# Seven-product up-projection of a transformer trunk: the first pair's products in another order, its first weight splits ahead of the activation sums, and the modulation's transposes one step later

## Chip, cores and metric

The kernel runs on one core of a Trainium2 chip. Times are device microseconds (us) of one execution. The core's engines are TensorE (PE, with its weight loads as PEld), VectorE (DVE), ScalarE (ACT), GpSimd (POOL) and SyncE (SP), which issues the DMA transfers. Each engine takes its instructions in order.

## What is computed

One inference step of a two-layer streaming encoder over 1024 prompt positions and 8 x 16 sample positions, model width 1024. Each layer has attention (of two kinds), then a GEGLU channel mixer with a causal convolution of width 3 between its projections. A modulation by `c` (shift, scale and gate, from a linear layer) goes around both. The part that matters here is the channel mixer:

```python
def conv_ffn(h, prev, w_up, conv_w, conv_b, w_down):
    u = h @ w_up
    B, T, C = u.shape
    if prev is None:
        prev = jnp.zeros((B, CONV_W - 1, C), u.dtype)
    ue = jnp.concatenate([prev.astype(u.dtype), u], axis=1)
    y = conv_b
    for tap in range(CONV_W):
        y = y + conv_w[tap] * ue[:, tap:tap + T]
    a, g = jnp.split(y, 2, axis=-1)
    out = (jax.nn.gelu(g) * a) @ w_down
    return out, ue[:, T:]
```

`h` has 1152 rows in all, `w_up` is 1024 x 5632 (22 column blocks of 128 for `a`, 22 for `g`), `w_down` 2816 x 1024. All is float32; a float32 product is made of three matmuls, with each operand split in a high and a low part (`hi`: a cast on ACT, L183; `lo`: a subtraction, mostly on DVE, L194): low times high, high times low, high times high.

## The kernel before

**Pairs.** In each layer, blocks j = 0 and 1 of the up-projection are plain matmuls (`plain`, L312). Blocks 2 to 21 are pairs (`spair`): the `a` and the `g` block of one j are seen as a 2x2 block matrix against a 2x2 split of the activations, and the eight products of such a multiplication are replaced by seven, on sums of blocks (`products`, L1229). A product is 24 matmuls, 12 for each of two column parts (320 and 256 columns), with weights of 128x512 split into `wh` and `wl`. Products 11, 21 and 22 of the first pair take activations as they are (in H); products 2, 3, 4 and 1 need sums of activations. Each product accumulates in one of three pairs of PSUM banks: 11 and 21 share one (21 adds on top of 11), 2, 3 and 4 share the second, 1 and 22 the third. `evict` reads them: product 11 is copied by ACT to `p1` (L1197), 21 by ACT (L1188, in `read`), the others are added by DVE (L1190). As product 21 adds to the bank of product 11, its matmuls wait for the copies of L1197.

**Sums.** `tsums` makes the sums of activations for nine tiles of 128 positions: SP loads the tile (`F<-hD`, L1131), POOL makes two subtractions (L1135, L1136), DVE two (L1137, L1138), and each of three results is split by a cast on ACT (into `xa` or `x2r`) and a subtraction on DVE. A fourth sum, T1S, is gathered over all tiles, and at the end of `tsums` split at once, into a part of H that products 11, 21 and 22 do not read, for product 1 (ACT 128x2304, then DVE). The weights of a pair (L1394, L1395, 512 KB each) are summed by POOL (L1177 to L1180) at the head of `products`, and the split of a product's weights is written ahead of its matmuls. Each of the wide casts and copies on ACT is thus in one queue: the sums' casts, the T1S cast, the weight casts, the convolution's L1299, the copies of L1197.

**Order.** The program is written as Python loops; a scheduling layer then sets each engine's order from the written order, data dependences and priorities (`issue_after`, `high_priority`), and inserts the waits. So a line that moves can shift the order elsewhere.

**Modulation.** `ada` is a generator that is advanced a step at a time (`self.step(1)`, at products 0, 2, 4 and 6 of a pair): sixteen weight loads with small matmuls (L240), two for each of eight steps, then a bias added by DVE (L259) and four transposes on PE (L267), in one step. Four of them run in layer 0's pairs and two in layer 0's attention.

**Tables.** After the first pair of layer 0, `tables_b` (L1789 to L1796) loads a table for the second layer's attention, works on it, writes it out (`eb`) and spreads it by sixteen transfers `skb<-eb` of 393 KB each. They go through SP's queue.

**After the pairs** of layer 1 follows the down-projection `down2` (L1604), whose weights (`in_wdn_dram`) and activations (`actD`) come by DMA. The convolution's ACT part of the last pair (L1340) reads and writes a PSUM bank.

Of the kernel before, what the change touches and what calls it, by code (L numbers as in the profile page):

```python
# [35 lines left out]
NPL = 2  # L36
# [69 lines left out]
class Trunk:  # L106
# [116 lines left out]
    def ada(self, gi, bank, ring=None):  # L223

        nc = self.nc
        ring = ring or self.ws
        ps = self.bank(bank)
        lead = [None] * 4
        for k in range(8):
            for hf in range(2):  # L230
                w = ring.next()
# [29 lines left out]
        if gate is not None:  # L261
            g, hf = gate
            nc.gpsimd.tensor_scalar_add(row[:, 512:768], row[:, hf * 256 : hf * 256 + 256], 1.0)
            for j in range(4):
                nc.sync.dma_start(self.gd[g, :, j * 256 : j * 256 + 256], row[32 * j : 32 * j + 9, 512:768])
        for i in range(4):
            nc.tensor.transpose(ps[:, i * 128 : i * 128 + 128], row[:, i * 128 : i * 128 + 128], self.ident)  # L267
        dst = self.adaT[:, gi * 144 : gi * 144 + 144].rearrange("p (h j i r) -> p h i j r", h=2, j=4, i=2)
# [857 lines left out]
    def tsums(self, ring, order, T1S, TT):  # L1126
        nc = self.nc
        E = nc.vector if len(TT) == 4 else nc.gpsimd
        for t in order:
            s = ring.next()  # L1130
            nc.sync.dma_start(s, self.hD[t])  # L1131
# [3 lines left out]
            E.tensor_sub(x1, b12, b11)  # L1135
            E.tensor_sub(b12, b22, b12)  # L1136
            nc.vector.tensor_sub(b22, b22, x1)  # L1137
            nc.vector.tensor_sub(b21, b21, b22)  # L1138
# [12 lines left out]

    def tviews(self):
# [1 line left out]
        TT = [(X1[:, 0:2304], X1[:, 2304:4608]), (X1[:, 4608:6912], X1[:, 6912:9216]), (X2[:, 0:2304], X2[:, 2304:4608])]  # L1154
        return [[x.rearrange("p (k n) -> p k n", k=4) for x in t] for t in TT]

    def products(self, sa, sg, ua, ug, S, p1s, sub, TT, after, when=None):
        nc = self.nc
        H5 = self.H.rearrange("p a c (t h i) -> p a c t h i", h=2, i=64)

# [13 lines left out]
        S1, S2, S3 = S  # L1174
        a11, a12, a21, a22 = sa[:, 0:512], sa[:, 512:1024], sg[:, 0:512], sg[:, 512:1024]
        E = nc.gpsimd
        E.tensor_add(S1, a21, a22)  # L1177
        E.tensor_sub(S2, S1, a11)
        E.tensor_sub(S3, a11, a21)
        E.tensor_sub(a21, a12, S2)  # L1180

        def read(d, a, ps, n):
            def v(x):
                x = x[:, 0 : NB[n][3] - NB[n][2]]
                return x.rearrange("p (t i) -> p t i", i=64)

            if a is None:
                nc.scalar.copy(d, v(ps))  # L1188
            else:
                nc.vector.tensor_add(d, v(ps), a if len(a.shape) == 3 else v(a))  # L1190

# [20 lines left out]
                if early:  # L1212
                    read(a1, a1, ps, n)

        src = {11: a11, 2: S2, 21: a12, 3: S3, 1: S1, 4: a22, 22: a21}
# [28 lines left out]
    def ffn(self, l, xsrc, xdst, affs):  # L1244
# [142 lines left out]
                    conv_block(ps, j, gg, bi, y[gg][:, bi * 384 : bi * 384 + 384])  # L1387
            gated(j, *y)

        sub = self.subslots(self.wslots[1:4] if l else self.wslots)  # L1390

        def spair(j):
            sa, sg = self.ws.next(), self.ws.next()
            nc.sync.dma_start(sa, I["wup"][l, j])  # L1394
            pairdma = nc.sync.dma_start(sg, I["wup"][l, j + 22]).ins  # L1395
# [16 lines left out]
            self.products(sa, sg, ua, ug, (S1, S2, S3), p1s, sub, TT, after, "first" if j == NPL else None)  # L1412
            ya = yact if l else ys.next()
            row(ua, j, 0, ya)
            gated(j, ya, y[0])
# [7 lines left out]
        self.ws = wide  # L1423
        if l == 0:
            self.bg = [self.ada(g, 7, wide) for g in (3, 4, 5, 6)]
        self.tsums(Ring([F[:, 1536:2560], F[:, 8700:9724], F[:, 11644:12668]]), (0, 1, 2, 3, 4, 8, 5, 6, 7), T1S, TT)
        for u in us.items:
            nc.gpsimd.memset(u[:, 0:2], 0.0)
        for j in range(NPL, NFF):
            spair(j)  # L1430
# [628 lines left out]
```

## Time and profile before

| | |
|---|---|
| median of three runs | 2764.85 us (2760.22 to 2769.29) |
| profiled execution | 2755.46 us, span 2753.7 us |
| mean granted TensorE clock | 0.988 |
| layer 0: plain blocks to pairs | about 524 us |
| layer 1: plain blocks to pairs | about 2026 us |
| layer 1: pairs to down-projection | about 2480 us |

A row of a timeline has start, duration, engine, line, operation, tiles (out <- in), shapes and count, and in brackets the idle time of the engine ahead of it with what ended it. A group's row has busy time and mean duration in ns behind the bar, then idle time ahead of its instructions. A row of waits has the total, the count and the longest. A row of stretches has the window, its length, the busy time of PE, PEld, DVE, ACT and POOL, the granted TensorE clock, the mean share of busy DMA engines and GB/s.

### The profile page before, as it was taken

The numbers are of one execution on the slowest core, as the hardware profiler recorded it, in microseconds if no ns is written. First come the engines' busy times: TensorE is split into PE (matmuls) and PEld (weight loads), VectorE is DVE, ScalarE is ACT, GpSimd is POOL, SyncE is SP. The second block draws the span as 40 slices with busy tenths as digits, with TensorE's granted clock in tenths as the row PEclk, the third lists the DMA queues.
The fourth block names the chain that finished last, engine by engine and source line by source line (L and its number), as shares of the span: only waits on it lengthen the run. The fifth ranks groups of instructions, "written<-read, shape, count | busy, mean of one in ns | idle before, by whom it ended". The sixth has DMA issues, their size and how long they took to land.

```text
span 2753.7 us, 47055 instructions
## 1 busy us (share of the span) xinstructions
PE 2642.9 (96%) x17266; PEld 2342.1 (85%) x17266; DVE 1924.2 (70%) x3836; ACT 1346.8 (49%) x2777; POOL 1066.5 (39%) x775
## 2 busy tenths in 40 slices
PE   7999889999999999999999999989999999998997
PEld 5997768989999998788898888867899999996886
DVE  4376768777666784867754677776787777777568
ACT  3476734433333453543536666662455444455553
POOL 3132623444443467764220121242467656542101
PEclk9999999999999999999999999999999999999999
DMA  8756444564444446765757457773544433348573
GB/s 293 237 159 200 146 132 157 163 233 150 145 149 156 137 141 226 246 212 184 274 200 265 113 158 193 215 216 115 176 147 167 150 135 132 134 152 277 192 240 122
DMA packets 229527, 498.27 MB, mean 181 GB/s; under 512 B 37456, under 2 KB 99232, under 8 KB 229296
## 3 DMA queue, kind: packets, MB, share of 16 engines
q1 hardware_dynamic: 229296, 495.27, 54.7%
q8 instruction: 136, 2.23, 0.3%
q14 instruction: 95, 0.78, 0.1%
HBM read 378.15 MB, written 126.47 MB: 183 GB/s over the span
## 4 chain that ended last, share of the span: by engine, by line
PE 36%; DVE 7%; DMA 3%; issue 2%; ACT 2%; POOL 1%; SPq 0%; DVEq 0%; ACTq 0%; POOLq 0%
PE PS L1229 14%; PE PS L1604 7%; PE PS L325 5%; PE PS L312 4%; PE PS L608 2%; PE PS L586 1%; PE PS L557 1%; DVE wl L194 1%; DVE F L524 1%; DMA w0f<-in_wdn_dram 1%; PE PS L560 1%; DVE xa L194 1%; PE PS L735 1%; DMA H<-actD 0%; DVE x2r L593 0%
## 5 line engine op out<-in xcount | busy, mean ns | idle before, releaser
L1229 PE MATMUL PS<-H,wh 128*128 128x256 f32 (+1 forms) x2288 | 352.8, 295 | 0.0
L1229 PEld LDWEIGHTS PS<-H,wh 128*128 128x128 f32 x2288 | 319.7, 189 | 0.4 <-issue 0.4
L1190 DVE TENSOR_TENSOR F<-PS,F 128x256 f32<-128x256 f32 (+1 forms) x446 | 197.7, 452 | 170.2 <-PE PS L1229 163.2
L183 ACT CAST wh<-F 128x512 fp32r<-128x512 f32 (+3 forms) x224 | 137.8, 625 | 209.7 <-PE PS L1229 94.1
L194 DVE TENSOR_TENSOR wl<-F,wh 128x512 fp32r<-128x512 f32 (+2 forms) x208 | 199.3, 968 | 42.3 <-ACT wh L183 41.7
L1229 PE MATMUL PS<-H,wl 128*128 128x256 f32 (+1 forms) x1144 | 201.8, 297 | 13.0 <-ACT F L1197 6.3
L1229 PEld LDWEIGHTS PS<-H,wl 128*128 128x128 f32 x1144 | 168.9, 190 | 19.0 <-ACT F L1197 6.5
L1229 PE MATMUL PS<-xa,wh 128*128 128x320 f32 (+1 forms) x1152 | 176.2, 294 | 0.0
L1229 PEld LDWEIGHTS PS<-xa,wh 128*128 128x128 f32 x1152 | 159.7, 188 | 0.4 <-issue 0.4
L1472 DVE TENSOR_TENSOR xa<-xa 128x384 fp32r<-128x384 f32 x66 | 97.5, 1489 | 78.2 <-ACT xa L183 74.8
L646 POOL TENSOR_TENSOR F<-F,x2r 64x512 f32<-64x512 f32 x62 | 79.3, 1279 | 163.3 <-DVE F L622 149.4
L1349 POOL TENSOR_TENSOR F<-F 128x1152 f32<-128x1152 f32 x44 | 124.2, 2822 | 47.1 <-DVE F L1342 27.6
L312 PE MATMUL PS<-H,w0r 128*128 128x384 f32 (+1 forms) x720 | 137.2, 341 | 0.0
L325 PE MATMUL PS<-xa,H 128*128 128x512 f32 x504 | 131.1, 402 | 6.2 <-ACT xa L183 3.3
L183 ACT CAST wh<-ws 128x512 fp32r<-128x512 f32 (+1 forms) x120 | 88.9, 747 | 96.0 <-PE PS L1229 39.9
L1278 DVE SCALAR_TENSOR_TENSOR F<-F 128x1024 f32<-128x1024 f32 (+2 forms) x160 | 130.1, 863 | 4.4 <-ACT F L1317 3.1
L312 PE MATMUL PS<-H,wh 128*128 128x384 f32 (+1 forms) x672 | 131.3, 339 | 0.0
L312 PEld LDWEIGHTS PS<-H,w0r 128*128 128x128 f32 x720 | 124.1, 188 | 2.8 <-issue 1.5
L586 PE MATMUL PS<-C,F 128*128 128x128 f32 x720 | 111.6, 279 | 14.6 <-DVE wh L593 5.8
L194 POOL TENSOR_TENSOR wl<-ws,wh 128x1024 fp32r<-128x1024 f32 x28 | 73.1, 2610 | 134.1 <-ACT wh L183 104.0
L325 PEld LDWEIGHTS PS<-xa,H 128*128 128x128 f32 x504 | 95.2, 192 | 28.6 <-ACT xa L183 3.8
L524 DVE CUSTOM_DVE_ANT_0 F<-PS,F,C 128x256 f32<-128x256 f32 (+3 forms) x208 | 97.4, 479 | 30.5 <-PE PS L560 15.0
(360 smaller groups left out, 6988.4 us busy)
## 6 DMA issues: line engine op xcount, KB each, us to landing
ws<-in_adaw_dram SPq DMA_DIRECT2D x64, 512.0 KB
ws<-in_wup_dram SPq DMA_DIRECT2D x49, 512.0 KB
F<-in_adaw_dram SPq DMA_DIRECT2D x48, 512.0 KB
F<-in_wup_dram SPq DMA_DIRECT2D x39, 512.0 KB
actD<-F SPq DMA_DIRECT2D x33, 576.0 KB
ws<-in_wdn_dram SPq DMA_DIRECT2D x33, 512.0 KB
F<-in_wdn_dram SPq DMA_DIRECT2D x33, 512.0 KB
xa<-kH SPq DMA_DIRECT2D x60, 256.0 KB
```

The source lines that it names most:

```text
L183: nc.scalar.copy(out, in_)
L194: self.eng(el).tensor_sub(lo, src, hi.bitcast(F32))
L312: mm = self.nc.tensor.matmul(out[:, 0:n], w[a][:, k * 128 : k * 128 + 128], H[:, p, k, s0 : s0 + n], start=i == 0, stop=i == 23)
L325: self.nc.tensor.matmul(out[:, 0:n], H[:, p, j * kn + k, t0 : t0 + 128], w[a][:, k * n : k * n + n], start=i == 0, stop=i == 23,)
L524: nc.vector.tensor_tensor_reduce(out=p[:, c0 : c0 + w], in0=ps, in1=b, scale=1.0, scalar=init, op0=ALU.add, op1=ALU.min, accum_out=nm)
L586: nc.tensor.transpose(t[:, n * 128 : n * 128 + 128], p[:, (kt - k0) * 128 : (kt - k0) * 128 + 128], self.ident)
L1190: nc.vector.tensor_add(d, v(ps), a if len(a.shape) == 3 else v(a))
L1229: self.pairmm = nc.tensor.matmul(ps[:, 0:m], w[a][:, k * 128 : k * 128 + 128], x(p, k, n), start=start and c == 0, stop=c == 11, skip_grou ...
L1278: nc.vector.scalar_tensor_tensor(o, u, cw[:, cc, i : i + 1], o, op0=ALU.mult, op1=ALU.add)
L1349: nc.gpsimd.tensor_mul(yg, yg, ya)
L1472: nc.vector.tensor_sub(lo, raw, hi.bitcast(F32))
L1604: self.downmm = nc.tensor.matmul(ps, a[p][:, i * 128 : i * 128 + 128], w[q], start=first and c == 0, stop=last and c == 2, skip_group_chec ...
```

## The change

The loads, sums and splits of the first pair's weights (products 11, 22, 21) are written ahead of `tsums`, the raw products run in the order 11, 22, 21, and the split of T1S is written behind product 21's matmuls, to be issued after its evacuation (`tplace`). Two memsets go from POOL to DVE, the first pair skips the modulation steps at its products 0 and 2, and `ada` gives way once more ahead of its transposes. The ring of weight slots starts with another slot. Lines from L267 on have other numbers: L1229 is now L1237, L1197 is L1204, L1188 is L1195, L1131 is L1132, L1299 is L1307, L1340 is L1348, L1604 is L1627, L1796 is L1819.

```diff
@@ ada
+        yield
         for i in range(4):
             nc.tensor.transpose(ps[:, i * 128 : i * 128 + 128], row[:, i * 128 : i * 128 + 128], self.ident)
@@ tsums
-        if len(TT) == 3:
-            H5 = self.H.rearrange("p a c (t h i) -> p a c t h i", h=2, i=64)
+
+    def tplace(self, T1S):
+        H5 = self.H.rearrange("p a c (t h i) -> p a c t h i", h=2, i=64)
+        with self.tc.issue_after(self.evac):
             self.split(T1S, H5[:, 0, 0:4, :, 1, :], H5[:, 1, 0:4, :, 1, :], "a", "v")
@@ products
+    def presum(self, sa, sg, S):
+        E = self.nc.gpsimd
+        S1, S2, S3 = S
+        a11, a12, a21, a22 = sa[:, 0:512], sa[:, 512:1024], sg[:, 0:512], sg[:, 512:1024]
+        E.tensor_add(S1, a21, a22)
+        E.tensor_sub(S2, S1, a11)
+        E.tensor_sub(S3, a11, a21)
+        E.tensor_sub(a21, a12, S2)
+        return {11: a11, 2: S2, 21: a12, 3: S3, 1: S1, 4: a22, 22: a21}
+
-    def products(self, sa, sg, ua, ug, S, p1s, sub, TT, after, when=None):
+    def products(self, sa, sg, ua, ug, S, p1s, sub, TT, after, when=None, src=None, ready={}):
...
+        src = src or self.presum(sa, sg, S)
...
             if a is None:
-                nc.scalar.copy(d, v(ps))
+                self.evac = nc.scalar.copy(d, v(ps)).ins
...
-        order = {None: (11, 2, 21, 3, 1, 4, 22), "first": (11, 21, 22, 2, 3, 1, 4), "last": (11, 2, 3, 1, 4, 21, 22)}[when]
+        order = {None: (11, 2, 21, 3, 1, 4, 22), "first": (11, 22, 21, 2, 3, 1, 4), "last": (11, 2, 3, 1, 4, 21, 22)}[when]
         for i, q in enumerate(order):
-            w = sub.next()
-            self.split(src[q], *w, "a", "v")
+            w = ready.get(q)
+            if w is None:
+                w = sub.next()
+                self.split(src[q], *w, "a", "v")
@@ ffn
-        sub = self.subslots(self.wslots[1:4] if l else self.wslots)
+        sub = self.subslots(self.wslots[3:4] + self.wslots[l:3])
...
-        def spair(j):
+        def spair(j, loaded=None, src=None, ready={}):
...
             def after(i, q):
-                if i % 2 == 0:
+                if j == NPL and i == 2:
+                    self.tplace(T1S)
+                    for u in us.items[1:3]:
+                        nc.vector.memset(u[:, 0:2], 0.0)
+                if i % 2 == 0 and (j > NPL or i > 2):
                     self.step(1)
...
+        first = pairload(NPL)
+        src = self.presum(first[0], first[1], (S1, S2, S3))
+        ready = {}
+        for q in (11, 22, 21):
+            ready[q] = sub.next()
+            self.split(src[q], *ready[q], "a", "v")
         self.tsums(Ring([F[:, 1536:2560], F[:, 8700:9724], F[:, 11644:12668]]), (0, 1, 2, 3, 4, 8, 5, 6, 7), T1S, TT)
-        for u in us.items:
-            nc.gpsimd.memset(u[:, 0:2], 0.0)
+        nc.gpsimd.memset(us.items[0][:, 0:2], 0.0)
```

The engines' orders at the three places that the prediction speaks of. First ACT in layer 1, where the sums end and the first pair begins; `x2r<-F` are casts of the sums, `H<-F 128x36x64` is the T1S cast, `wh<-` are weight casts. Before:

```order
L1299 ACTIVATE F<-PS,F 128x384
L183 CAST x2r<-F 128x4x64
L1291 COPY F<-PS 128x18
L183 CAST x2r<-F 128x4x64
L183 CAST H<-F 128x36x64
L183 CAST wh<-ws 128x512
L1299 ACTIVATE F<-PS,F 128x384
L183 CAST wh<-F 128x512
L1197 COPY F<-PS 128x320
L1197 COPY F<-PS 128x256
```

And with the change, the same place:

```order
L183 CAST x2r<-F 128x4x64
L183 CAST wh<-F 128x512
L1307 ACTIVATE F<-PS,F 128x384
L183 CAST wh<-F 128x512
L1204 COPY F<-PS 128x320
L1204 COPY F<-PS 128x256
L183 CAST wh<-ws 128x512
L1299 COPY F<-PS 128x18
L1356 ACTIVATE F<-F 128x1152
L183 CAST wh<-F 128x512
L1195 COPY F<-PS 128x5x64
L1195 COPY F<-PS 128x4x64
```

The T1S cast has left the rows ahead of the copies of product 11 (L1197, now L1204); it stands directly behind the last row shown, the evacuation of product 21 (L1195). In layer 0 the two copies stand directly behind the last cast of the sums.

Second, SP's queue in layer 0, from the last loads of the sums (`F<-hD`) to the weights of the second pair (`in_wup_dram`). Before:

```order
L1131 DMA F<-hD 128x1024 x2
L232 DMA ws<-in_adaw_dram 128x1024
L1131 DMA F<-hD 128x1024
L1351 DMA actD<-F 128x1152
L232 DMA F<-in_adaw_dram 128x1024 x2
L1789 DMA F<-in_relf_dram 16x257
L1394 DMA F<-in_wup_dram 128x1024
L1351 DMA actD<-F 128x1152
L1792 DMA eb<-F 16x768
L1395 DMA ws<-in_wup_dram 128x1024
L232 DMA F<-in_adaw_dram 128x1024
L1796 DMA skb<-eb 128x1x768 x10
```

With the change:

```order
L1812 DMA ws<-in_relf_dram 16x257
L1132 DMA F<-hD 128x1024
L1815 DMA eb<-ws 16x768
L1132 DMA F<-hD 128x1024
L232 DMA ws<-in_adaw_dram 128x1024
L1819 DMA skb<-eb 128x1x768 x3
L1132 DMA F<-hD 128x1024
L1359 DMA actD<-F 128x1152
L1819 DMA skb<-eb 128x1x768 x3
L232 DMA F<-in_adaw_dram 128x1024
L1819 DMA skb<-eb 128x1x768 x4
L232 DMA F<-in_adaw_dram 128x1024
```

The table's load and the `skb` transfers, which stood behind the second pair's weights, now stand between the last loads of the sums and ahead of those weights (fourteen of the sixteen are ahead of the first one).

Third, PE in layer 1 where the last pair ends and `down2` begins. Before (the last two rows are the last product of the pair, its second column part):

```order
L1229 MATMUL PS<-x2r,wh 128x256 x8
L1229 MATMUL PS<-H,wl 128x320 x4
L1229 MATMUL PS<-H,wh 128x320 x8
L1604 MATMUL PS<-wh,xa 128x512 x3
L1604 MATMUL PS<-wl,xa 128x512
L1604 MATMUL PS<-wh,xa 128x512
...
L1604 MATMUL PS<-wh,xa 128x512
L1229 MATMUL PS<-H,wl 128x256 x4
L1229 MATMUL PS<-H,wh 128x256 x8
```

With the change:

```order
L1237 MATMUL PS<-x2r,wh 128x320 x8
L1627 MATMUL PS<-wh,xa 128x512
L1627 MATMUL PS<-wl,xa 128x512
L1237 MATMUL PS<-x2r,wl 128x256 x4
L1237 MATMUL PS<-x2r,wh 128x256 x8
L1237 MATMUL PS<-H,wl 128x320 x4
L1237 MATMUL PS<-H,wh 128x320 x8
L1627 MATMUL PS<-wh,xa 128x512 x2
...
L1627 MATMUL PS<-wh,xa 128x512
L1237 MATMUL PS<-H,wl 128x256 x4
L1237 MATMUL PS<-H,wh 128x256 x8
```

Two of `down2`'s matmuls now stand ahead of the last two groups of the pair, and 58 more (12 before) ahead of its last twelve matmuls.

More of the change, by code (lines that the diff above doesn't have):

```diff
@@ L1172, in halves @@
             return v.rearrange("p (t h i) -> p t h i", h=2, i=64)[:, :, h, :]
[L1174 to L1180, printed above, removed]
+        src = src or self.presum(sa, sg, S)
         def read(d, a, ps, n):
@@ L1213, in evict @@
                     read(a1, a1, ps, n)
-        src = {11: a11, 2: S2, 21: a12, 3: S3, 1: S1, 4: a22, 22: a21}
         group = {11: 0, 21: 0, 2: 1, 3: 1, 4: 1, 1: 2, 22: 2}
-        order = {None: (11, 2, 21, 3, 1, 4, 22), "first": (11, 21, 22, 2, 3, 1, 4), "last": (11, 2, 3, 1, 4, 21, 22)}[when]
+        order = {None: (11, 2, 21, 3, 1, 4, 22), "first": (11, 22, 21, 2, 3, 1, 4), "last": (11, 2, 3, 1, 4, 21, 22)}[when]
         for i, q in enumerate(order):
-            w = sub.next()
-            self.split(src[q], *w, "a", "v")
+            w = ready.get(q)
+            if w is None:
+                w = sub.next()
+                self.split(src[q], *w, "a", "v")
             x = operand(q)
@@ L1388, in plain, with pairload @@
             gated(j, *y)
-        sub = self.subslots(self.wslots[1:4] if l else self.wslots)
-        def spair(j):
+        sub = self.subslots(self.wslots[3:4] + self.wslots[l:3])
+        def pairload(j):
             sa, sg = self.ws.next(), self.ws.next()
             nc.sync.dma_start(sa, I["wup"][l, j])
-            pairdma = nc.sync.dma_start(sg, I["wup"][l, j + 22]).ins
+            return sa, sg, nc.sync.dma_start(sg, I["wup"][l, j + 22]).ins
+        def spair(j, loaded=None, src=None, ready={}):
+            sa, sg, pairdma = loaded or pairload(j)
             ua, ug = us.next(), us.next()
@@ L1410, in after @@
                     row(ug, j, 1, y[0])
-            self.products(sa, sg, ua, ug, (S1, S2, S3), p1s, sub, TT, after, "first" if j == NPL else None)
+            self.products(sa, sg, ua, ug, (S1, S2, S3), p1s, sub, TT, after, "first" if j == NPL else None, src, ready)
             ya = yact if l else ys.next()
@@ L1425, in ffn @@
             self.bg = [self.ada(g, 7, wide) for g in (3, 4, 5, 6)]
+        first = pairload(NPL)
[4 more added lines that the diff above has]
+            self.split(src[q], *ready[q], "a", "v")
         self.tsums(Ring([F[:, 1536:2560], F[:, 8700:9724], F[:, 11644:12668]]), (0, 1, 2, 3, 4, 8, 5, 6, 7), T1S, TT)
-        for u in us.items:
-            nc.gpsimd.memset(u[:, 0:2], 0.0)
+        nc.gpsimd.memset(us.items[0][:, 0:2], 0.0)
         for j in range(NPL, NFF):
-            spair(j)
+            if j == NPL:
+                spair(j, first, src, ready)
+            else:
+                spair(j)
             if l == 0 and j == 2:
```

## Prediction

> **What bounds the kernel now.** I start on the profile's page, with the busy shares.
>
> ```profile
> span 2753.7 us, 47055 instructions
> PE 2642.9 (96%) x17266; PEld 2342.1 (85%) x17266; DVE 1924.2 (70%) x3836; ACT 1346.8 (49%) x2777; POOL 1066.5 (39%) x775
> L1229 PE MATMUL PS<-H,wl 128*128 128x256 f32 (+1 forms) x1144 | 201.8, 297 | 13.0 <-ACT F L1197 6.3
> ```
>
> TensorE (PE) works 96% of the span, so only its 111 us of idle time (2753.7 - 2642.9), and time at a reduced clock, can be won; the other engines count where PE waits for them. The second row is a group of the seven-product matmuls: the last column says that it lost 13.0 us to idle time, 6.3 of it to the copy on ACT at L1197. The waits grouped by what PE waited for (total, times, longest) show where this comes from.
>
> ```profile
> PE PS L1229 <- ACT F L1197: 8.5, 2, 6.3
> PE PS L1229 <- ACT PS L1340: 5.2, 1, 5.2
> ```
>
> So the copies at L1197 (product 11's evacuation, on whose bank product 21 accumulates) cost two waits, one in each layer's first pair. Next the timeline of PE and ACT (start, duration) at the first, in layer 0.
>
> ```profile
> 523.80 3.04 PE L1229 MATMUL PS<-H,w0r 128*128 128x320 f32 x22
> 526.68 0.75 PE L1229 MATMUL PS<-H,wl 128*128 128x320 f32 x4
> 532.06 4.98 PE L1229 MATMUL PS<-H,w0r 128*128 128x320 f32 x24 [2.20 <-ACT F L1197]
> 536.88 0.28 PE L1229 MATMUL PS<-H,wh 128*128 128x256 f32 x1
> 527.67 0.41 ACT L183 CAST x2r<-F 128x256 fp32r<-128x256 f32 x1
> 527.98 2.12 ACT L183 CAST H<-F 128x2304 fp32r<-128x2304 f32 x1
> 531.59 0.69 ACT L1197 COPY F<-PS 128x320 f32<-128x320 f32 x2
> ```
>
> The copies stand in ACT's queue behind the last cast of the activation sums (527.67) and the 2.12 us cast that splits T1S (527.98). PE has products 11 and 22 and then stands 2.20 us. The 24 matmuls behind the wait take 532.06 to 536.88, 4.82 us; ahead of it 22 of the same took 2.88 (523.80 to the next group's start at 526.68), so 24 would take 3.14. The other 1.68 us are a slower clock: the table of stretches gives it (the number behind POOL's), here and in layer 1.
>
> ```profile
> 532.00:536.00 4.00, 3.94 (x17) 3.94 (x18) 3.66 (x8) 0.55 (x4) 0.36 (x3) 0.58 0.00 0
> 2036.00:2042.00 6.00, 6.00 (x27) 6.00 (x28) 5.54 (x8) 1.27 (x4) 5.38 (x7) 0.55 0.10 21
> ```
>
> Granted clock 0.58 and 0.55, after 2.20 and 6.29 us of idle time. The Trainium skill, "TensorE: Matmul & The Clock Gate", section "What's actually happening", puts the fall to half clock behind an idle window of about 3.4 us; by that, the 2.20 us wait would cost no clock and the sum below would be 1.7 us smaller. The row of 0.58 differs, and I go by it.
>
> Layer 1 is the same place with a dearer wait:
>
> ```profile
> 2026.33 0.74 PE L1229 MATMUL PS<-H,wl 128*128 128x320 f32 x4
> 2028.56 1.10 PE L1229 MATMUL PS<-H,wh 128*128 128x256 f32 x8
> 2035.96 1.44 PE L1229 MATMUL PS<-H,wl 128*128 128x320 f32 x4 [6.29 <-ACT F L1197]
> 2041.65 0.75 PE L1229 MATMUL PS<-H,wl 128*128 128x320 f32 x4
> 2031.57 0.41 ACT L183 CAST x2r<-F 128x256 fp32r<-128x256 f32 x1 [0.16 <-DVE F L1138]
> 2031.88 2.11 ACT L183 CAST H<-F 128x2304 fp32r<-128x2304 f32 x1
> 2033.89 0.61 ACT L183 CAST wh<-ws 128x512 fp32r<-128x512 f32 x1
> 2034.41 0.67 ACT L1299 ACTIVATE F<-PS,F 128x384 f32<-128x384 f32 x1
> 2034.98 0.61 ACT L183 CAST wh<-F 128x512 fp32r<-128x512 f32 x1
> 2035.49 0.69 ACT L1197 COPY F<-PS 128x320 f32<-128x320 f32 x2
> ```
>
> Here only product 11 (24 matmuls, 2026.33 to 2029.66) is there to run; then 6.29 us of nothing, then 24 matmuls in 5.69 us (2035.96 to 2041.65) where 3.33 is normal: 2.36 of clock.
>
> **The change, part by part.** All sums are made against the profiled execution, 2755.46 us; it lies 9.4 under the median of the runs, 2764.85, to which the differences are then applied.
>
> *Layer 1, -7.4.* The T1S cast goes behind product 21's evacuation and product 22 ahead of 21. On ACT there remain, behind the cast of 2031.57, one weight cast, one L1299 and one more weight cast, then the copies. From row to row those three take 1.60 us (2033.89 to 2035.49); so the copies start at 1.6 behind 2031.95 or so, 2033.6, and PE, which started 0.47 after the copies' start (2035.49 to 2035.96), at 2034.0. Its two products now reach from 2026.33 to 2033.0 (twice 3.33). A wait of 1.0 to 1.1 stays, half of what first brought a slow clock above. Saved: 6.29 - 1.1 + 2.36 = 7.55. The T1S split, 2.11 on ACT and as much again on DVE, now stands between the evictions of products 21 and 2, where PE has two products (6.7 us) before it needs what is behind; I take 0.15 of new waiting, bounds 0 and 1.5.
>
> *Layer 0, -3.2.* Products 11 and 22 already ran ahead of 21, so PE needs the copies at 523.80 + 2 x 3.14 = 530.1. The last cast of the sums ended at 528.08, and the copies now follow it directly: with 0.47 to PE that is 528.6, 1.5 us early, if the last tile comes as before. It may not, for the next reason, so 0.7 of wait is taken: -(2.20 - 0.7 + 1.68) = -3.2, bounds -3.9 and 0.
>
> *The skew loads, -3.0.* A side effect: the tables of the second attention now use a weight slot, and their sixteen `skb<-eb` loads stand in SP's queue among the last loads of the sums. Before:
>
> ```profile
> 510.54 3.29 SPq L1131 DMA_DIRECT2D F<-hD  x2
> 518.94 0.32 SPq L1131 DMA_DIRECT2D F<-hD  x1
> 524.77 0.75 POOL L1135 TENSOR_TENSOR F<-F 128x256 f32<-128x256 f32 x1 [3.00 <-DMA F<-hD]
> 538.80 0.33 SPq L1789 DMA_DIRECT2D F<-in_relf_dram  x1
> 539.27 0.33 SPq L1394 DMA_DIRECT2D F<-in_wup_dram  x1
> 545.86 7.75 SPq L1796 DMA_DIRECT2D skb<-eb  x10
> 545.00:573.00 28.00, 26.39 (x216) 24.46 (x215) 17.60 (x29) 8.34 (x15) 10.90 (x7) 1.00 0.97 323
> 578.04 1.47 POOL L1177 TENSOR_TENSOR F<-F 128x512 f32<-128x512 f32 x1 [13.09 <-DMA F<-in_wup_dram]
> 567.27 0.64 PE L240 MATMUL PS<-ws,C 128*32 128x256 f32 x8 [1.61 <-DMA ws<-in_adaw_dram]
> 579.29 0.64 PE L240 MATMUL PS<-F,C 128*32 128x256 f32 x8 [0.68 <-DMA F<-in_adaw_dram]
> 581.38 0.85 PE L1229 MATMUL PS<-H,wl 128*128 128x320 f32 x4 [1.46 <-DVE wl L194]
> ```
>
> They held the DMA engines at 0.97 and 323 GB/s for 28 us, and behind them POOL waited 13.09 us for the third pair's weights and PE 1.61 + 0.68 + 1.46 = 3.75. Started some 25 us earlier, they fall where DMA had gaps: in 532 to 536 the row above has 0.00. I take 3.0 of the 3.75, bounds 0 and -3.75. The price is on the other side: three of the skb loads (393 KB each, 3.65 us at 323 GB/s) now stand ahead of the last load of the sums, which so far took 5.8 us from issue to use (518.94 to 524.77); that is the 0.7 above. Pair 2's weights stand behind fourteen of them, but at that rate these take 17 us from about 520, which ends before the 539.27 at which the first of them was issued so far.
>
> *Layer 1's last pair and the down-projection, -4.5.* The instruction order moves here too, though the diff touches nothing near. Before, the last pair's last twelve matmuls stood 12 matmuls into the down-projection and waited 5.2 us (L1340, quoted).
>
> ```profile
> 2481.10 0.96 PE L1604 MATMUL PS<-wh,xa 128*128 128x512 f32 x3 [1.59 <-ACT wh L183]
> 2490.69 1.19 PE L1229 MATMUL PS<-H,wl 128*128 128x256 f32 x4 [5.23 <-ACT PS L1340]
> 2490.00:2500.00 10.00, 8.60 (x28) 7.17 (x29) 7.40 (x14) 6.03 (x10) 2.37 (x4) 0.56 0.90 289
> 2483.10 0.33 SPq L1588 DMA_DIRECT2D w0f<-in_wdn_dram  x1
> ```
>
> Now 58 down-projection matmuls stand ahead of them, enough to cover the 5.23; and with it would go the clock of 0.56 behind it, worth at most 8.60 x 0.44 = 3.8. Together 9.0. But those 58 need their weights that much earlier, and DMA is at 0.90; and PE now meets the first of them two matmul groups sooner. I take half, -4.5, bounds -9 and +3 (a first weight that lands with the load of 2483.10 instead of by 2481.10, plus 1 of clock).
>
> *Modulation.* Six times, the transposes stand one step later. The four in layer 0's pairs are read only in later stages. The two in layer 0's attention move past other work, so that PE's order differs through that stage; the wait for them was 2.0 in all:
>
> ```profile
> PE PS L267 <- DVE ws L259: 2.0, 1, 2.0
> ```
>
> Behind it stand other waits for DVE, so I count +1, bounds -2 and +4. The moved weight loads, presum and casts of the first pair cost PE nothing, since it runs the plain blocks meanwhile.
>
> **Sum:** -7.4 - 3.2 - 3.0 - 4.5 + 1 = -17.1: the profiled execution would be 2738.4, the median **2747.8 us**.
>
> **Rivals.** (1) *The wait comes back at product 21*, because the last tile's load is late. For it: the loads queued ahead. The Trainium skill, "DMA: Bandwidth & Descriptors", section "Queues, rings and completion order", has each DMA engine take descriptors in ring order from the one row that SP owns; by that the three skb loads would be paid in full. The 13.09 above agrees as far as it goes. With 3.65 us of delay, less 1.5 of slack, layer 0 waits 2.2 as before and keeps the slow clock (0 saved); if layer 1's 1.1 also grows to 2.2 and meets the slow clock, it saves 4.1. With nothing at the down-projection: -4.1 - 3.0 + 1 = -6, or 2759.
>
> (2) *The down-projection gives its whole 9 us:* 4.5 more, 2743. Against it stands DMA at 0.90.
>
> (3) *Slower:* SP's queue stands at the skb loads until `eb` has landed, which needs the relf load and two DVE instructions that now sit among those of the sums; all that is behind, the last load of the sums first, is late by X. Before, relf's chain had SP to itself. Each us over 1.5 is a us of PE at product 21, and some 3.8 of clock come with a long wait; against the 3.9 of today layer 0 then loses X - 1.6. With the skew and down-projection terms nil, layer 1's 7.4 is used up at X = 9, and 0.3% is passed at X = 17. At X = 20 that is -7.4 + 18.4 = +11, 2776. Against it: the whole chain from relf's issue to the first skb took 7.1 us before (538.80 to 545.86), and relf's load now stands ahead of the seventh of the sums' nine loads, which was issued at 510.54: from there the chain ends at 517.6, ahead of 518.94.
>
> (4) *It does nothing*: T1S's split, now ahead of product 2's eviction and of the next weight casts, makes PE wait behind product 21 for as long as it waited ahead of it. It would take 17 us of new waits in the pair; all that is moved there is, in each layer, 2.11 us on ACT and about as much on DVE. Within 0.3%, at 2762.
>
> **How the numbers follow.** Forecast with its terms 0.52, rival 2 0.13, rival 1 0.20, rival 4 0.08, rival 3 0.07. Half of rival 1 lies within 0.3% (8.3 us, about what a measurement of this kernel can tell from no change), and of the forecast's own spread a tenth. So faster 0.70, same 0.23, slower 0.07. The range goes from rival 2 with attention's -2, layer 0's 0.7 and the skew's 0.75 (2738) to rival 1 with 5 more for the spread of the median (2764).
>
> **What would show it.** Layer 1: no wait over 1.5 us at product 21 around 2034 less what was won earlier, clock 1.0 behind it. Layer 0: the copies directly behind the last cast; if the last L1132 load lands over 1.5 us later than 5.8 us after 518.9, rival 1 or 3. The waits of 567 to 581 are gone if the skew term holds; the 5.23 is gone if the last does. I am wrong if a new wait of over 3 us shows in the first pairs, or at the first down-projection matmul.

## The result, and the profile after

The changed kernel takes 2746.43 us (median of 8 runs), the kernel before 2759.56 (8 runs, three of them those of the prediction): ratio 0.9945, interval 0.993 to 0.9961, so 15 us less (the two medians differ by 13.1). The forecast was 17.1 less. The time is about as forecast; the places where it was won are not, and the rest of this document is about that.

First the page of the changed kernel, as before:

```profile
span 2743.6 us, 47063 instructions
PE 2639.7 (96%) x17266; PEld 2339.8 (85%) x17266; DVE 1936.4 (71%) x3840; ACT 1350.6 (49%) x2777; POOL 1069.0 (39%) x771
```

PE's idle time fell from 110.8 to 103.9 us (2743.6 - 2639.7). What it waits for, grouped (total, times, longest):

```profile
PE PS L1237 <- DVE wl L194: 5.8, 3, 4.0
PE PS L1237 <- DVE F L1197: 5.3, 6, 1.3
PE PS L240 <- DMA F<-in_adaw_dram: 3.1, 1, 3.1
PE PS L1237 <- ACT F L1204: 2.8, 2, 2.4
```

The wait for the copies of product 11 (L1204, was L1197) fell from 8.5 to 2.8; L1197 in the second row is, in this kernel, DVE's addition in `read`, which was L1190. The 5.2 for L1340 (now L1348) has no row any more. But waits of 4.0 for a weight split and 3.1 for a modulation weight are new. To see what each stage gained, I take the start of the same matmul in both traces (counted: a pair has 168 product matmuls, the down-projection 1056) and follow the difference, changed minus before:

| at the start of | difference, us | step |
|---|---|---|
| layer 0, first product | +2.89 | +2.89 |
| layer 0, product matmul 48 | +0.39 | -2.50 |
| layer 0, second pair | +2.37 | +1.98 |
| layer 0, fourth pair | +0.34 | -2.03 |
| layer 0, last product matmul | +4.11 | +3.77 |
| layer 1, first product | +4.85 | +0.74 |
| layer 1, product matmul 48 | -1.70 | -6.55 |
| layer 1, second pair | +5.29 | +6.99 |
| layer 1, 60 matmuls ahead of the pairs' end | +5.00 | -0.29 |
| down-projection, matmul 60 | -7.08 | -12.08 |
| end | -10.10 | -3.02 |

The first pairs, for which the edits are written, bring little: layer 1 wins 6.55 and loses 6.99, layer 0 is 2.55 ahead at its fourth pair and loses 3.77 in the later ones. One stretch, where the diff touches nothing, makes more than the whole difference: 12.08 us between the last pair and the 60th matmul of the down-projection.

**Layer 1, first pair.** The timelines of PE, ACT, POOL, DVE and SP's queue, changed kernel:

```profile
2031.18 0.75 PE L1237 MATMUL PS<-H,wl 128*128 128x320 f32 x4
2039.95 0.85 PE L1237 MATMUL PS<-H,wl 128*128 128x320 f32 x4 [2.35 <-ACT F L1204]
2050.51 1.41 PE L1237 MATMUL PS<-H,wl 128*128 128x320 f32 x4 [4.04 <-DVE wl L194]
2037.57 0.41 ACT L183 CAST x2r<-F 128x256 fp32r<-128x256 f32 x1 [0.16 <-DVE F L1139]
2039.47 0.70 ACT L1204 COPY F<-PS 128x320 f32<-128x320 f32 x2
2045.95 1.16 ACT L1356 ACTIVATE F<-F 128x1152 f32<-128x1152 f32 x1 [3.02 <-POOL F L1295]
2047.02 0.60 ACT L183 CAST wh<-F 128x512 fp32r<-128x512 f32 x1
2043.04 1.44 POOL L1166 TENSOR_TENSOR F<-F 128x512 f32<-128x512 f32 x1 [8.56 <-DMA F<-in_wup_dram]
2045.69 0.23 POOL L1295 TENSOR_TENSOR F<-F 128x16 f32<-128x16 f32 x1
2047.65 2.72 DVE L194 TENSOR_TENSOR wl<-F,wh 128x512 fp32r<-128x512 f32 x1 [3.60 <-ACT wh L183]
2027.65 0.50 SPq L1402 DMA_DIRECT2D ws<-in_wup_dram  x1
2036.68 0.33 SPq L1403 DMA_DIRECT2D F<-in_wup_dram  x1
```

The first part went as worked out: the copies start 1.90 behind the last cast's start (2037.57, 2039.47; forecast 2.0), and PE 0.48 after them. 2.35 us stay instead of 1.1, mostly because the sums as a whole ended 1.15 later against PE (the last cast at 2031.57 and 2037.57, the first product at 2026.33 and 2031.18); also, two products take 6.4 us, where the forecast counted twice 3.33. The second wait was not foreseen. Read from PE back: product 1's weights wait for their subtraction on DVE (2047.65, 2.72 us), this for the cast on ACT (2047.02), this stands in ACT's queue behind the gelu of the last plain block (2045.95), this waits for a 0.23 us addition on POOL (2045.69), and that stands in POOL's queue behind sums of the second pair's weights, which waited 8.56 us for their load (the second pair's two loads are the last two rows). Before, PE was 6 us later here and none of this showed.

**Layer 0, first pair.** PE, ACT and SP's queue:

```profile
532.70 3.29 PE L1237 MATMUL PS<-H,w0r 128*128 128x320 f32 x24
542.19 1.07 PE L240 MATMUL PS<-F,C 128*32 128x256 f32 x16 [3.07 <-DMA F<-in_adaw_dram]
544.08 2.33 PE L1237 MATMUL PS<-xa,wh 128*128 128x320 f32 x8
561.99 2.48 PE L1237 MATMUL PS<-H,w0r 128*128 128x320 f32 x16 [1.42 <-DVE w0r L194]
532.11 0.70 ACT L1204 COPY F<-PS 128x320 f32<-128x320 f32 x2
518.19 1.86 SPq L1819 DMA_DIRECT2D skb<-eb  x3
522.90 0.33 SPq L1132 DMA_DIRECT2D F<-hD  x1
531.34 0.34 SPq L232 DMA_DIRECT2D F<-in_adaw_dram  x1
532.27 5.50 SPq L1819 DMA_DIRECT2D skb<-eb  x4
```

Product 21 (532.70) starts without a wait, 24 matmuls in 3.29 us at full clock: the 2.20 and the 1.68 are gone. The last load of the sums was issued at 522.90 instead of 518.94, but the copies were just in time. Then PE waits 3.07 us for a modulation weight whose load was issued among the skb transfers, and eight matmuls take 2.33 us (544.08) that take 1.33 at full clock.

**End of layer 1's pairs.** PE, and the table of stretches:

```profile
2483.64 1.33 PE L1237 MATMUL PS<-H,wh 128*128 128x320 f32 x8
2484.81 0.63 PE L1627 MATMUL PS<-wh,xa 128*128 128x512 f32 x2
2498.11 0.63 PE L1237 MATMUL PS<-H,wl 128*128 128x256 f32 x4
2500.36 0.97 PE L1627 MATMUL PS<-wh,xa 128*128 128x512 f32 x3 [0.71 <-ACT wh L183]
2485.00:2490.00 5.00, 5.00 (x23) 4.08 (x23) 5.00 (x10) 4.93 (x10) 0.00 (x0) 1.00 0.94 296
2490.00:2500.00 10.00, 9.65 (x49) 7.97 (x47) 8.85 (x15) 4.34 (x8) 0.22 (x1) 1.00 0.79 252
```

Through the 58 matmuls moved ahead PE does not stop, at clock 1.00; only 0.71 us of wait are left, which stood there before too.

### The profile page after: what moved, and what is told of

Same layout as the page of the kernel before. It is cut to its first block, busy times and chain, and to the rows that moved or that the text cites. A ratio compares the mean times of both kernels' runs of the same rounds, so it can differ in the third digit from the quotient of the medians.

```text
span 2743.6 us, 47063 instructions
## 1 busy us (share of the span) xinstructions
PE 2639.7 (96%) x17266; PEld 2339.8 (85%) x17266; DVE 1936.4 (71%) x3840; ACT 1350.6 (49%) x2777; POOL 1069.0 (39%) x771
## 4 chain that ended last, share of the span: by engine, by line
PE 38%; DVE 6%; DMA 3%; issue 1%; ACT 1%; POOL 1%; SPq 0%; DVEq 0%; POOLq 0%; ACTq 0%
PE PS L1237 14%; PE PS L1627 9%; PE PS L326 5%; PE PS L313 4%; PE PS L609 2%; PE PS L587 2%; DVE wl L194 1%; PE PS L558 1%; PE PS L561 1%; DVE F L525 1%; PE PS L736 1%; DVE xa L194 0%; DVE F L1197 0%; DMA F<-in_cvB_dram 0%; DVE PS L1286 0%
## 5 line engine op out<-in xcount | busy, mean ns | idle before, releaser
L1237 PE MATMUL PS<-H,wh 128*128 128x256 f32 (+1 forms) x2304 | 352.4, 294 | 0.0
L1237 PEld LDWEIGHTS PS<-H,wh 128*128 128x128 f32 x2304 | 319.8, 188 | 0.0
L1197 DVE TENSOR_TENSOR F<-PS,F 128x256 f32<-128x256 f32 (+1 forms) x446 | 196.9, 451 | 165.1 <-PE PS L1237 155.7
L194 DVE TENSOR_TENSOR wl<-F,wh 128x512 fp32r<-128x512 f32 (+2 forms) x205 | 197.1, 972 | 44.1 <-ACT wh L183 40.6
L1237 PE MATMUL PS<-H,wl 128*128 128x320 f32 (+1 forms) x1152 | 202.3, 296 | 7.3 <-DVE wl L194 4.4
L1237 PEld LDWEIGHTS PS<-H,wl 128*128 128x128 f32 x1152 | 169.6, 189 | 13.7 <-issue 4.8
L1237 PE MATMUL PS<-xa,wh 128*128 128x320 f32 (+1 forms) x1168 | 179.8, 295 | 0.0
L1237 PEld LDWEIGHTS PS<-xa,wh 128*128 128x128 f32 x1168 | 163.1, 189 | 0.0
L194 POOL TENSOR_TENSOR wl<-ws,wh 128x1024 fp32r<-128x1024 f32 x28 | 73.5, 2626 | 124.9 <-ACT wh L183 87.7
L326 PE MATMUL PS<-wh,H 128*128 128x512 f32 (+1 forms) x468 | 117.8, 360 | 0.5 <-ACT wh L183 0.5
```

The source lines that it names most:

```text
L194: self.eng(el).tensor_sub(lo, src, hi.bitcast(F32))
L326: self.nc.tensor.matmul(out[:, 0:n], H[:, p, j * kn + k, t0 : t0 + 128], w[a][:, k * n : k * n + n], start=i == 0, stop=i == 23,)
L1237: self.pairmm = nc.tensor.matmul(ps[:, 0:m], w[a][:, k * 128 : k * 128 + 128], x(p, k, n), start=start and c == 0, stop=c == 11, skip_grou ...
```

## The experiments

Theory A: the gain is the order at the end of layer 1's pairs; the edits at the first pairs give nothing, since each wait removed comes back a product later. Theory B: the prediction's terms. All ratios are to the kernel before, from runs on the same chip in the same session.

### One line of the change alone: e1_ring_only

The order at the end of layer 1's pairs moves in the same way when only this line is changed:

```diff
-        sub = self.subslots(self.wslots[1:4] if l else self.wslots)
+        sub = self.subslots(self.wslots[3:4] + self.wslots[l:3])
```

> The kernel before with one line of the change alone: the ring of weight slots starts with slot 3. It changes the order at the end of layer 1's pairs as the whole change does (58 down-projection matmuls ahead of the last twelve product matmuls instead of 12). Theory A (the gain comes from that order, the first pairs give nothing): 10 to 13 us faster than before, waits of 1.60, 1.06 and 5.23 us at 2480 to 2491 and the half clock of 10.2 us gone. Theory B (the prediction's terms: this place gives 4.5, the first pairs more): 3 to 6 us faster.

Measured: 2745.12 us, ratio 0.9934 (0.9914 to 0.9954). The step at the pairs' end is -12.08, as in the changed kernel, and the last twelve product matmuls no longer wait there:

```profile
2481.55 1.33 PE L1229 MATMUL PS<-H,wh 128*128 128x320 f32 x8
2496.02 0.63 PE L1229 MATMUL PS<-H,wl 128*128 128x256 f32 x4
2496.49 1.07 PE L1229 MATMUL PS<-H,wh 128*128 128x256 f32 x8
```

The first pairs still wait for the copies of L1197:

```profile
539.60 0.84 PE L1229 MATMUL PS<-H,wl 128*128 128x320 f32 x4 [0.88 <-ACT F L1197]
2041.44 1.43 PE L1229 MATMUL PS<-H,wl 128*128 128x320 f32 x4 [4.14 <-ACT F L1197]
```

0.88 and 4.14 instead of 2.20 and 6.30: in layer 1 the scheduling layer now puts product 22 ahead of 21 by itself. This one line gives at least as much as the whole change (0.9945); the intervals overlap. Theory A, with more than its 10 to 13 us (16 by the medians, 18 by the ratio): besides the 12 us, the profile shows 4.3 won in layer 0's first three pairs, where the order moved too and no half clock follows the shorter wait.

### All of the change but that line: e2_all_but_ring

```diff
-        sub = self.subslots(self.wslots[3:4] + self.wslots[l:3])
+        sub = self.subslots(self.wslots[1:4] if l else self.wslots)
```

> The changed kernel with the old start of the ring, so with the old order at the end of layer 1's pairs; everything else of the change is in. Theory A: no faster than before, between 3 us faster and 5 us slower, with a wait of about 4 us at product 1 of layer 1's first pair and the 5.23 us wait for L1348 back. Theory B: 8 to 12 us faster.

Measured: 2769.37 us, ratio 1.0026 (1.001 to 1.0042): slower than before. The waits of PE:

```profile
2498.51 1.20 PE L1237 MATMUL PS<-H,wl 128*128 128x256 f32 x4 [5.23 <-ACT PS L1348]
2589.61 4.63 PE L1627 MATMUL PS<-H 128*128 128x512 f32 x10 [8.12 <-DVE x2f L1681]
```

The 5.23 is back. The 8.12 is new, in the down-projection, where this kernel's order differs again; the step there is +10.8 us. Without it the kernel would stand some 4 us under before, between the theories' numbers but nearer to A's. The wait at product 1 of layer 1 is 1.75 here, not 4, and product 21 waits 3.32 for its weights instead; over the first three pairs of layer 0 and the first two of layer 1 the kernel is 1.1 and 0.2 us slower than before. So this run confirms where the 12 us are from, and shows that any edit can move the order in a far stage by as much; as a price of the remaining edits it is not clean.

### Without the added yield: e3_no_yield

```diff
-        yield
         for i in range(4):
             nc.tensor.transpose(ps[:, i * 128 : i * 128 + 128], row[:, i * 128 : i * 128 + 128], self.ident)
```

> The changed kernel without the added yield (modulation transposes in the same step as before). Theory: the yield costs 3 us in layer 0's attention, so this is 3 us faster than the changed kernel, 18 under before, and the first product of layer 0 starts 2 to 3 us earlier. Rival: the attention's order is set by something else and nothing moves by over 1 us.

Measured: 2747.67 us, ratio 0.9951 (0.9934 to 0.9968), the same as the changed kernel; the first product starts at +4.35 us against before, not earlier. The yield costs nothing that can be measured. That the +2.89 of the table need be no cost of an edit shows in other runs too: in the next one (e4) every engine's order up to layer 0's first pair is that of the kernel before, in e1 up to about 499 us, and their first products start at +5.78 and +9.20; at 456 us e1 was 9.2 us behind already. The table of stretches for layer 0's attention, kernel before:

```profile
215.00:310.00 95.00, 90.16 (x761) 76.13 (x750) 62.56 (x222) 60.31 (x174) 26.14 (x25) 1.00 0.61 188
310.00:400.00 90.00, 73.75 (x515) 54.34 (x516) 62.19 (x187) 44.55 (x111) 40.27 (x33) 0.96 0.37 111
```

and e1_ring_only, with the same order there:

```profile
215.00:310.00 95.00, 89.05 (x743) 74.71 (x740) 60.63 (x215) 57.37 (x169) 24.86 (x24) 0.98 0.59 187
310.00:400.00 90.00, 74.66 (x510) 54.47 (x511) 56.63 (x183) 46.84 (x121) 38.06 (x32) 0.89 0.39 112
```

The granted clock is 1.00 and 0.96 in one profile, 0.98 and 0.89 in the other.

### The product order alone: e4_order_only

```diff
-        order = {None: (11, 2, 21, 3, 1, 4, 22), "first": (11, 21, 22, 2, 3, 1, 4), "last": (11, 2, 3, 1, 4, 21, 22)}[when]
+        order = {None: (11, 2, 21, 3, 1, 4, 22), "first": (11, 22, 21, 2, 3, 1, 4), "last": (11, 2, 3, 1, 4, 21, 22)}[when]
```

> The kernel before with the product order 11, 22, 21 in the first pairs alone; the T1S split stays ahead of the copies. Theory B: product 22 fills 3.3 of layer 1's 6.3 us and the slow clock goes: 5 us faster. Theory A: the wait returns at the next product whose weights come late; 0 to 2 us faster, with a new wait of 2 us or more at product 2, 3 or 1.

Measured: 2764.51 us, ratio 1.0008 (0.9994 to 1.0021): no change. In layer 1 product 22 does run in the gap, but the wait behind it is hardly shorter:

```profile
2046.71 1.41 PE L1229 MATMUL PS<-H,wl 128*128 128x320 f32 x4 [5.82 <-DVE wl L194]
```

As theory A has it, only that the wait is at product 21 itself, for its weights' subtraction on DVE, and not at a later product.

### The chain behind the new wait in layer 1: e5_sums_behind_edge

`edge` is the last plain block's addition on POOL (L1295); in layer 1 the second pair's sums go behind it.

```diff
-        src = src or self.presum(sa, sg, S)
+        if src is None:
+            with self.tc.issue_after(hold) if hold else ExitStack():
+                src = self.presum(sa, sg, S)
...
-            self.products(sa, sg, ua, ug, (S1, S2, S3), p1s, sub, TT, after, "first" if j == NPL else None, src, ready)
+            self.products(sa, sg, ua, ug, (S1, S2, S3), p1s, sub, TT, after, "first" if j == NPL else None, src, ready, edge if l and j == NPL + 1 else None)
```

> The changed kernel, with POOL's four weight sums of layer 1's second pair ordered behind the last plain block's small edge addition. Theory: the new 4.04 us wait at product 1 of layer 1's first pair hangs on a chain (second pair's weight load, POOL's sums, edge addition, gelu, weight cast, its subtraction); with the edge addition ahead of the sums it falls under 1.5 us, the half clock of 6.8 us goes, and the kernel is 4 to 6 us faster than the changed one. Rival: the cast waits for a weight slot or for product 21's copies, and the wait stays over 3 us.

Measured: 2745.69 us, ratio 0.9935 (0.9919 to 0.995): not told apart from the changed kernel. The waits of PE in layer 1's first two pairs:

```profile
2039.98 0.98 PE L1239 MATMUL PS<-H,wl 128*128 128x320 f32 x4 [2.19 <-ACT F L1206]
2060.59 0.85 PE L1239 MATMUL PS<-H,wl 128*128 128x320 f32 x4 [0.78 <-DVE wl L194]
2068.84 0.70 PE L1239 MATMUL PS<-H,wl 128*128 128x256 f32 x4 [1.29 <-DVE F L1344]
2077.23 0.85 PE L1239 MATMUL PS<-H,wl 128*128 128x320 f32 x4 [0.82 <-DVE wl L194]
```

The chain was right, the 4.04 us wait is gone. The price was not: three shorter waits stand behind it, up to the second pair's end, where the changed kernel has none over 0.4 us, and from layer 1's first product to its third pair this kernel needs 0.9 us less than before; the changed one needed 0.7 more (+4.85 to +5.53).

### The skew transfers, one per pair: e6_skew_spread

The `issue_after` in the code names a PE instruction, and as the orders of SP show, all sixteen transfers stand within the first pairs. Here it names an instruction of SP:

```diff
             sa, sg, pairdma = loaded or pairload(j)
+            self.pairdma = pairdma
...
-                with self.tc.issue_after(self.pairmm):
+                with self.tc.issue_after(self.pairdma):
                     self.skew_b(j - 3)
```

> The changed kernel, with each of the sixteen skb transfers ordered in SP's queue behind the weight loads of another pair (pairs 2 to 17) instead of all at once. Theory: the 3.07 us wait for a modulation weight in layer 0's first pair and its half clock come from the skb transfers ahead of that load; they go, as do the waits in the second pair: 4 to 7 us faster than the changed kernel. Rival: the modulation load waits for its buffer, not for the transfers; under 2 us.

Measured: 2740.70 us, ratio 0.9912 (0.9896 to 0.9928); by the ratios 9 us under the changed kernel (0.0033 of 2760), by the medians 6; the intervals do not overlap. In layer 0's first three pairs PE waits only here:

```profile
530.17 2.03 PE L1237 MATMUL PS<-H,w0r 128*128 128x320 f32 x12 [0.75 <-ACT F L1204]
533.52 1.64 PE L1237 MATMUL PS<-H,w0r 128*128 128x256 f32 x12 [1.32 <-ACT F L1204]
```

From matmul 48 to the fourth pair it gains 6.5 us on before (-0.97, -4.71, -0.82), where the changed kernel gained nothing (+1.98, -2.03). The theory holds, at or above the upper end of its 4 to 7 us.

### Both: e7_both

> Both of these edits in one kernel. If they are independent, the sum: 8 to 12 us faster than the changed kernel, about 2737 us, ratio to before about 0.991.

Measured: 2741.71 us, ratio 0.9922 (0.9907 to 0.9938). The edge edit adds nothing that can be measured to the spread transfers (e6, 0.9912). Against the changed kernel it is 5 us by the medians and 6 by the ratios, under the 8 to 12 of the sum; the expected ratio of 0.991 lies within the interval, so the sum is not excluded.

### The ring's start and the spread transfers alone: e8_ring_skew

The kernel before with the two lines of e1 and e6, and none of the moved splits, order or T1S.

> The kernel before with the ring's start and the spread skb transfers alone (nothing of the moved splits, order and T1S). If the moved splits give nothing of their own, this equals the changed kernel with spread transfers within 3 us; if they give 5 us or more once the later waits are gone, it is slower than that by as much.

Measured: 2737.77 us, ratio 0.9905 (0.989 to 0.9921), the lowest median of all, though not told apart from e6. In layer 1 it still waits at the place that the change was written for:

```profile
2035.25 1.24 PE L1229 MATMUL PS<-H,wl 128*128 128x320 f32 x4 [4.32 <-ACT F L1197]
```

and needs 0.6 us less than before from layer 1's first product to its third pair (-1.75 to -2.32). So the moved splits, order and T1S give nothing of their own even where the skb transfers no longer stand in their way.

### The modulation as before: e9_modulation_back and e10_skew_modulation_back

The table has +3.77 in the later pairs of layer 0. The modulation's last transposes, at 954.61 before, now stand at 988.24, with more of its matmuls (L240) ahead of them, and behind them two waits are new (0.95 and 0.99 us, around 990); one around 1022 is 0.88 instead of 0.67. Both kernels undo this, e9 on the changed kernel, e10 on e6:

```diff
-        yield
         for i in range(4):
...
-                if i % 2 == 0 and (j > NPL or i > 2):
+                if i % 2 == 0:
                     self.step(1)
```

> The changed kernel with the modulation as before: no added yield, and its steps run from the first pair's product 0 on. Theory: the two steps skipped push the end of layer 0's modulation from 955 to 988 us, into the last pairs, where 0.95, 0.99 and 0.88 us waits for DVE's additions are new; with the steps back, the stretch from the tenth to the last pair is 3 to 5 us shorter, and the kernel 2 to 4 us faster than the changed one. Rival: the same work only sits elsewhere; within 1.5 us.

> The changed kernel with the spread skb transfers and the modulation as before. If both effects hold and add: 6 to 13 us faster than the changed kernel, about 2736 us and a ratio to before near 0.990. If it equals the kernel with the ring's start and the spread transfers alone (0.9905) within its interval, the moved splits, the product order and the late T1S split give nothing.

Measured: e9 2747.01 us, ratio 0.9958 (0.9943 to 0.9973); e10 2747.93 us, 0.9952 (0.9937 to 0.9966). The later pairs did get shorter (from the tenth pair's end to the last matmul +0.1 us against before in e9 and -0.1 in e10, the changed kernel +4.9), but in e9 the first three pairs lost 2.9 against the changed kernel, and both kernels have a new wait there, here e10's:

```profile
540.27 0.64 PE L240 MATMUL PS<-F,C 128*32 128x256 f32 x8 [3.59 <-ACT F L1298]
```

So the two skipped steps pay in the first pairs and cost about as much later. e10 misses what was expected of it both ways: it is no faster than the changed kernel, 0.4% slower than e6 and 0.5% slower than e8. The profiles don't say why: up to the end of layer 0's pairs e10 and e6 differ by 0.6 us from the first product on, and layer 1's attention takes 6.2 us longer in e10, with the granted clock at one half for 20.5 us in it and for 13.7 in e6.

## Why the prediction came out right, and which steps were wrong

By the sign that the prediction gave for being wrong, a new wait of over 3 us in the first pairs, it was wrong: there are two, 4.04 and 3.07. That the total agrees is luck.

**Layer 1, -7.4: wrong, +0.4.** The wait and clock at product 21 were forecast well (3.9 of the 6.3 us went, and no slow clock followed the 2.35 that stayed), and the 6.55 won up to that point shows it. The step that failed is "I take 0.15 of new waiting, bounds 0 and 1.5". I looked only at what the T1S split itself would hold up. With PE 6 us earlier, the next thing in line was late: product 1's weights, through ACT's and POOL's queues, behind the second pair's load. It cost 4.04 us and a slow clock (four and eight matmuls in 2050.51 to 2053.85, 3.34 us, where 1.76 is normal). e5, e4 and e8 show that the stage gives next to nothing whichever wait is taken away: in all twelve profiles the third pair starts 52.4 to 54.5 us behind the first product (before: 53.5). Another thing is the same in all twelve: SP holds the second load of the second pair's weights (2036.68, 9 us behind the load ahead of it) until one of the sums' last subtractions on DVE is done, and issues it 4.4 to 5.6 us behind the first product. No run moves that load, so whether it sets the end of these pairs is open.

**Layer 0, -3.2: right.** The copies were in time, without the 0.7 that I left: -2.50 up to matmul 48, and the 1.68 of slow clock behind it are gone too. (Product 11 begins at 523.51; the row that I read, 523.80, starts with its third matmul, so the slack was 1.3 and not 1.5.)

**The skew loads, -3.0: wrong sign of the effect.** The step "Started some 25 us earlier, they fall where DMA had gaps" failed: the waits of 567 to 581 went, and a wait of 3.07 with a slow clock, then 1.42 and smaller ones, came in their place, so the stretch from matmul 48 to the fourth pair is as long as before although 1.68 us of slow clock are gone from it: +1.6 and not -3.0. Spread out, the transfers make this stretch 6.5 us shorter than in the changed kernel (e6), but only 3.5 shorter than with the heap at its old place (e1 -3.03, e8 -6.51 against before), close to the 3.75 that I read there: moving the heap forward made it dearer. The row that I needed was quoted: 13.09 us of waiting behind the transfers. I priced the queue for the last load of the sums and for pair 2's weights, and not for the modulation weight in the same queue. The Trainium skill's rule ("DMA: Bandwidth & Descriptors", section "Queues, rings and completion order", descriptors taken in ring order), cited for rival 1, agrees with this: PE had the load issued at 531.34 only 10.85 us later (542.19).

**The down-projection, -4.5: right kind, size off, -12.1.** Two errors. I counted 5.23 and its slow clock, and left out the 1.59 and 1.06 us waits ahead of it, which the same order removes. And "I take half", for DMA at 0.90: DMA was at 0.94 and 0.79 while the 58 matmuls ran, and no matmul waited for it. A row with a resource's share says nothing of whether the loads that are needed next are already there.

**Modulation, +1: +3.8 in the later pairs.** The yield costs nothing that can be measured (e3); the two skipped steps had no term in the sum. "Are read only in later stages", which made the late end free, failed: the steps that moved behind the tenth pair bring work and waits there, and save about the same in the first pairs (e9).

The forecast of -17.1 against -15.2 is thus errors of opposite sign: too much gain was forecast at layer 1's first pair (by 7.8 us), at the skew loads (4.6) and at the modulation (2.8), too little at the down-projection (7.6) and at layer 0's first pair (1.0), and 3 behind the down-projection were not foreseen. (The two profiles differ by 10.1 only, as the attention stages took 3.6 us more in the profile after, see the last section.) The forecast of 2747.8 also counted from a median of three runs, 2764.85, that is 5.3 above the median of eight. Rival 2 (the whole 9 us) came true and more, and of rival 4 the outcome at layer 1's pairs, but not its mechanism: the split of T1S delayed nothing that PE waited for. Rivals 1 and 3 did not decide: the last load of the sums was issued 4 us later, PE came 2.9 us later too, and it cost nothing. What the remaining edits cost or give by themselves is not settled: e2 holds another order in the down-projection, e6 and e8 overlap, and e10, which adds the moved splits, order and T1S to e8, is 0.5% slower, in the profiles mostly in layer 1's attention.

## What to carry to other kernels

Where a wait on the busiest engine is removed, follow its next three or four inputs as far back as their loads, each through the queue it stands in, and ask when they were ready and not only that nobody waited for them. Compare the two instruction orders over the whole program before the diff is weighed: here one ring's start moved 46 matmuls in a stage that the diff doesn't touch, and that was most of the gain. An order request that names an instruction of another engine may order nothing; look whether the transfers went where it says.

## What was not expected of the hardware

With the same order on every engine up to layer 0's first pair (in e1 up to about 499 us), that pair's first product started at 523.51 us in the profile of before, and at 532.71 and 529.29 in those of e1 and e4. The half clock up to 530 us (without the start) sums to 10.2, 30.7 and 23.9 us in the three, so the kernel before was profiled in a mild execution: 2755.46 us, against a median of 2759.56. Half of the additional half-clock time, 10.2 and 6.9 us, is about what the two are later (9.2 and 5.8). A difference of under 10 us between two profiles in that stage need not be the effect of an edit.

The slow clock does not follow from the length of one wait. 2.35 us at 2037.6 in the changed kernel brought none; 2.20 at 529.9 before did. Where the wait lies decides more. In each of the twelve profiles every change of the granted clock lies on a grid of 3.41 us. The 2.20 lay within one step of it (529.3 to 532.7, PE busy 35%), and the clock fell at that step's end; the 2.35 was divided by a border at 2038.7 (PE busy 69% and 62%). Counted over the twelve profiles, the clock fell behind 99 of the 100 full-clock steps with PE busy under 45%, behind 37 of the 110 with 45 to 60%, and behind 3 of the 9141 above that.

DVE's large subtractions can be much longer while POOL works: the one at 2047.65 took 2.72 us beside a product on POOL, and one of the same shape 0.67 at 2040.04, when POOL was idle. In the kernel before, 259 such subtractions (128x512, L194) ran beside an idle POOL, in 0.67 to 0.70 us each; 70 ran beside a POOL that was busy for over 95% of the time, in 0.67 to 2.98, the median being 1.11.
